# A gated FFN with seven block products for eight, GpSimd sums, and modulation on TensorE

## The chip, the cores and the metric

The kernel runs on one core of one Trainium2 chip. The metric is the device time of one execution in microseconds (us); less is better.

## The reference, cut to what matters

One inference step of a two-layer trunk for 128 context tokens and 512 latent tokens, D_MODEL 1024, all in float32. The change touches two parts of it: the up-projection of the FFN, 1024 to 2 x 2816, and the modulation vectors, six of 1024 per layer and condition.

```python
def adaln_params(cond, w_mod, b_mod):
    m = jax.nn.silu(cond) @ w_mod + b_mod
    return [t[:, None, :] for t in jnp.split(m, 6, axis=-1)]
def modulate(x, g, shift, scale):
    return rmsnorm(x, g) * (1 + scale) + shift
def conv_ffn(h, lp):
    gate, val = jnp.split(h @ lp["w_up"], 2, axis=-1)
    gate = dwconv(gate, lp["ffn_conv_w"], lp["ffn_conv_b"], FFN_CONV_PAD_L)
    return (jax.nn.gelu(gate) * val) @ lp["w_down"]
def layer(x, cond, lp, ctx):
    sh1, sc1, g1, sh2, sc2, g2 = adaln_params(cond, lp["w_mod"], lp["b_mod"])
    mix, ctx_out = token_mixers(modulate(x, lp["norm1_g"], sh1, sc1), lp, ctx)
    x = x + g1 * mix
    x = x + g2 * conv_ffn(modulate(x, lp["norm2_g"], sh2, sc2), lp)
    return x, ctx_out
```

## The kernel before, in words

Activations lie feature by feature: a chunk is 128 features in the partitions by 640 token columns (128 context, 512 latent), and 1024 features are eight chunks. TensorE works in a reduced float32 format, so every operand is split in a high and a low part, and `mm3` (358) makes three matmuls of each product: high by high, high by low, low by high. ScalarE writes the high part, VectorE the low one by a subtraction. `gemm` (367) makes one output chunk for half of the tokens (320 columns): 8 blocks of 128 input features x 3 matmuls into one of three PSUM banks `G`.

The FFN (`ffn`, 1355) goes over 22 pairs of a gate chunk and a value chunk. The first three gates are made by `first` (380) as h comes out of the norm. For every other chunk `wload` (287) fetches 512 KB of weights through a ring of two places and splits them. A gate chunk is copied out by ScalarE (`ffn_gate`, 1325), convolved and put through GeLU (`ffn_gelu`, 1341: one pass of ScalarE, two of VectorE, two of ScalarE), multiplied by the value bank (VectorE, 1385) and split. After a group of pairs (`FF_GROUPS`: 8, 8 and 6) `staggered` (1257) multiplies that group's part of W_down: eight output chunks by two halves, the last two chunks half by half, and `residual` (1247) adds the bank times the gate g2 to x, which stays in SBUF through the FFN.

The modulation vectors are made in three ways. Those of the first norm of layer 0 are part of `start` (1428). The second norm's shift and scale of layer 0 are made by `mods` (451) on TensorE: silu(c) is the stationary operand, four column tiles of 32 take four 512-column strips of w_mod at a time, in eight steps, then four transposes. The other eight vectors are made by `mods_rows` (516) on VectorE: for each of 128 (chunk, condition) pairs a row of w_mod times silu(c) is summed along 1024 columns. `mod_stream` (1594) does this for seven of the eight, within the FFN of layer 0: g2 of layer 0, then the six of layer 1; the other, g1 of layer 0, is in the attention stream.

What sets the order: TensorE's is the order of the Python text. `drive` (239) steps several generators by a model time of TensorE; `yield` gives a stream's next time or a mark that it waits for. The side streams (attention, recurrent mixer, modulation) go before the main one when they are due. The other engines and SP's DMA queue are ordered by a scheduler by priority: `soon` raises what frees a bank. Places in SBUF are handed out by hand from two pools, `F` (22 of 648 columns) and `R` (38).

The core of the modulation by rows, lines 532 to 537:

```python
for i in range(2):
    with self.soon(self.MLOW):
        nc.vector.scalar_tensor_tensor(
            out=self.S, in0=w.ap, scalar=1.0, in1=self.cb[i].ap, op0=ALU.mult, op1=ALU.mult,
            accum_out=self.mod[:, l, j, i : i + 1],
        )
```

## Time and profile before

| what | us |
|---|---|
| three runs | 2415.4 to 2415.9, median 2415.58 |
| profiled execution: span from the first to the last instruction | 2408.8 |
| median of the runs less that span | 6.8 |
| TensorE busy | 2377.8 |
| VectorE busy | 1596.7 |
| ScalarE busy | 1006.4 |
| GpSimd busy | 17.9 |

The profile has the span of the profiled execution and no total beside it; 6.8 us lie between the span and the median of the runs. Busy time is the union of an engine's instructions. TensorE's matmuls overlap (one lasts about 0.31 us and the next starts 0.15 us later), so what a matmul costs is read from the distance between starts.

### The profile page before, as it was taken

How to read it: one execution, taken by the hardware profiler on the slowest of the kernel's cores; microseconds unless marked ns; L12 is line 12 of the kernel's file. 1: busy time of each engine (PE TensorE's matmuls, PEld its weight loads, DVE VectorE, ACT ScalarE, POOL GpSimd, SP SyncE). 2: the span in 40 equal slices, each digit the busy share in tenths (PEclk: the TensorE clock that was granted, in tenths of full speed). 3: DMA queues.
4: the chain of work that ended last, by engine and by line, in shares of the span. 5: the costliest groups of instructions: out<-in, count | busy, mean ns of one | idle time of the engine just before them, and what ended most of it. 6: DMA issues, size and time to landing. Idle time of an engine off the chain costs nothing.

```text
span 2408.8 us, 41835 instructions
## 1 busy us (share of the span) xinstructions
PE 2377.8 (99%) x16847; PEld 2301.7 (96%) x16847; DVE 1596.7 (66%) x3054; ACT 1006.4 (42%) x1958; POOL 17.9 (1%) x190
## 2 busy tenths in 40 slices
PE   8999999999999999999999999999999999999998
PEld 7899999998999999999999999999889999999998
DVE  6588878766766667686756688777568564344345
ACT  4237565733334322313343566565233343133232
POOL 0000000000000000000000000000000000000000
PEclk8999999999999999999999999999999999999999
DMA  8752222222452444354423222222227212222222
GB/s 284 237 191 73 83 79 76 88 75 79 146 183 75 138 140 151 130 167 148 147 87 131 89 92 70 83 85 87 69 68 230 80 62 71 79 76 73 79 68 76
DMA packets 124961, 267.73 MB, mean 111 GB/s; under 512 B 12240, under 2 KB 45536, under 8 KB 124768
## 3 DMA queue, kind: packets, MB, share of 16 engines
q1 hardware_dynamic: 124768, 265.07, 33.2%
q8 instruction: 132, 2.16, 0.4%
q14 instruction: 61, 0.50, 0.1%
HBM read 236.95 MB, written 28.07 MB: 110 GB/s over the span
## 4 chain that ended last, share of the span: by engine, by line
PE 86%; DVE 6%; ACT 3%; DMA 3%; issue 2%; SPq 0%; DVEq 0%; ACTq 0%
PE g L273 72%; PE s L273 4%; PE tb L273 4%; PE pv L273 3%; PE tb L277 3%; DVE wl L299 1%; DMA f<-in_wmodt 1%; DVE s L534 1%; ACT f L1091 1%; PE pv L277 1%; DMA f<-in_wmod 0%; DMA wr<-in_woc 0%; DVE f L1252 0%; ACT f L913 0%; DVE r L616 0%
## 5 line engine op out<-in xcount | busy, mean ns | idle before, releaser
L273 PE MATMUL g<-r,wh 128*128 128x320 f32 (+1 forms) x7920 | 1768.5, 312 | 2.9 <-ACT f L1148 0.9
L273 PEld LDWEIGHTS g<-r,wh 128*128 128x128 f32 x7920 | 1316.6, 188 | 20.5 <-issue 13.1
L273 PE MATMUL g<-r,wl 128*128 128x320 f32 (+1 forms) x3960 | 1222.3, 309 | 2.7 <-DVE wl L299 2.7
L273 PEld LDWEIGHTS g<-r,wl 128*128 128x128 f32 x3960 | 745.1, 188 | 3.8 <-DVE wl L299 3.8
L299 DVE TENSOR_TENSOR wl<-wr,wh 128x1024 fp32r<-128x1024 f32 (+2 forms) x291 | 334.8, 1151 | 224.5 <-ACT wh L296 219.6
L296 ACT CAST wh<-wr 128x1024 fp32r<-128x1024 f32 (+2 forms) x201 | 194.2, 966 | 494.9 <-PE g L273 424.4
L1252 DVE SCALAR_TENSOR_TENSOR f<-g,mod,f 128x128 f32<-128x128 f32 (+3 forms) x192 | 78.3, 435 | 138.7 <-PE g L273 138.6
L534 DVE SCALAR_TENSOR_TENSOR s<-f 128x1024 f32<-128x1024 f32 x128 | 157.2, 1228 | 15.8 <-DMA f<-in_wmodt 11.3
L891 DVE TENSOR_REDUCE sm<-s 128x1 f32<-128x640 f32 (+3 forms) x104 | 92.8, 892 | 89.1 <-PE s L273 88.6
L273 PE MATMUL g<-r 128*128 128x322 f32 (+3 forms) x632 | 124.2, 315 | 1.4 <-ACT f L1166 1.0
L273 PE MATMUL g<-wh,r 128*128 128x256 f32 x576 | 107.7, 282 | 0.0
L273 PEld LDWEIGHTS g<-r 128*128 128x128 f32 x632 | 100.4, 190 | 5.6 <-ACT f L1091 2.1
L1385 DVE TENSOR_TENSOR f<-f,g 128x320 f32<-128x320 f32 x88 | 42.5, 486 | 91.7 <-PE g L273 56.1
L659 ACT CAST r<-f 128x640 fp32r<-128x640 f32 (+2 forms) x98 | 70.3, 720 | 65.7 <-PE s L273 27.0
L273 PEld LDWEIGHTS g<-wh,r 128*128 128x128 f32 x576 | 90.4, 188 | 3.4 <-issue 3.4
L273 PE MATMUL s<-k,r 128*128 128x320 f32 (+3 forms) x448 | 92.3, 326 | 0.9 <-ACT k L787 0.9
L660 DVE TENSOR_TENSOR r<-f,r 128x640 fp32r<-128x640 f32 (+2 forms) x98 | 79.1, 812 | 15.8 <-ACT r L659 8.4
L913 ACT ACTIVATE f<-s,sm,rs 128x640 f32<-128x640 f32 (+1 forms) x80 | 63.5, 796 | 62.0 <-DVE sm L895 44.9
L1348 DVE SCALAR_TENSOR_TENSOR f<-f,vec 128x641 f32<-128x641 f32 x88 | 77.8, 887 | 13.6 <-ACT f L1346 8.4
L913 ACT ACTIVATE f<-s,sm 128x384 f32<-128x384 f32 (+2 forms) x80 | 45.6, 577 | 92.8 <-DVE sm L900 71.0
L273 PE MATMUL g<-wl,r 128*128 128x256 f32 x288 | 81.1, 282 | 0.0
L277 PE MATMUL tb<-ident,f 128*128 128x128 f32 x576 | 79.7, 272 | 0.0
(202 smaller groups left out, 2472.6 us busy)
## 6 DMA issues: line engine op xcount, KB each, us to landing
wr<-in_wup SPq DMA_DIRECT2D x84, 512.0 KB, 3.2
wr<-in_win SPq DMA_DIRECT2D x77, 512.0 KB, 3.3
f<-in_wmodt SPq DMA_DIRECT2D x64, 512.0 KB, 4.1
f<-in_wmod SPq DMA_DIRECT2D x64, 256.0 KB, 4.6
wr<-in_wdown SPq DMA_DIRECT2D x32, 512.0 KB, 3.4
wr<-in_wqkv SPq DMA_DIRECT2D x24, 512.0 KB, 3.6
g_kept<-f SPq DMA_DIRECT2D x32, 320.0 KB, 2.3
f<-g_kept SPq DMA_DIRECT2D x32, 320.0 KB, 3.7
```

Source lines behind the costliest of these rows:

```text
L273: self.nc.tensor.matmul(**kw)
L277: self.nc.tensor.transpose(out, in_, self.ident)
L296: nc.scalar.copy(wh[:, :n], raw[:, :n])
L299: self.sub_engine().tensor_tensor(out=wl[:, o : o + c], in0=raw[:, o : o + c], in1=wh[:, o : o + c].bitcast(F32), op=ALU.subtract)
L534: nc.vector.scalar_tensor_tensor(out=self.S, in0=w.ap, scalar=1.0, in1=self.cb[i].ap, op0=ALU.mult, op1=ALU.mult, accum_out=self.mod[:, l, ...
L659: nc.scalar.copy(xh[:, :n], t[:, :n])
L660: (eng or nc.vector).tensor_tensor(out=xl[:, :n], in0=t[:, :n], in1=xh[:, :n].bitcast(F32), op=ALU.subtract)
L891: nc.vector.tensor_reduce(out=m_[:, lo:hi], in_=src, axis=AX.XY if hi - lo == 1 else AX.X, op=ALU.max)
L913: nc.scalar.activation(out=p[:, :n].rearrange("p (a c) -> p a c", a=2) if hi - lo == 1 else p[:, o : o + n], in_=src if hi - lo == 1 else ...
L1252: self.nc.vector.scalar_tensor_tensor(out=dst[:, lo:hi], in0=b[:, lo - c0 : hi - c0], scalar=self.mod[:, l, gate + m, i : i + 1], in1=src[ ...
L1348: nc.vector.scalar_tensor_tensor(out=g[:, :n], in0=gp[:, k : k + n], scalar=fw(k), in1=g[:, :n], op0=ALU.mult, op1=ALU.add)
L1385: nc.vector.tensor_tensor(out=gp[:, lo:hi], in0=gp[:, lo:hi], in1=b, op=ALU.mult)
```

## The change

The 2 x 2 block form of a pair's product: the weights of gate j and value j by the two halves of the input features, times h by halves of the features and of the tokens. Eight block products become seven, with sums of weight blocks and of h made before (by GpSimd) and sums of the products made after (by VectorE, from the banks). Three pairs of each layer stay plain (`PLAIN`). Six PSUM banks serve the products in turn. The groups become five of 5, 4, 4, 4 and 5 pairs. x no longer stays in SBUF during the FFN: it is stored at its start, read again by every group and stored by all but the last. Two weights of the down-projection are split before the group's last pair ends (`lead_weights`), and their products take all but the last block first (`gemms`). Seven modulation vectors go through `mods` on TensorE: g2 of layer 0 in its up-projection, layer 1's in the down-projection stages of layer 0's first four groups, 16 chunks (shift and scale) or 8 (a gate) at a time.

```diff
-FF_GROUPS = ((0, 8), (8, 8), (16, 6))
+FF_GROUPS = ((0, 5), (5, 4), (9, 4), (13, 4), (17, 5))
+PLAIN = 3
...
+    def gemms(self, jobs, xs, evac):
+        banks = [self.G.popleft() for _ in jobs]
+        n = len(xs)
+        for ks in (range(n - 1), (n - 1,)):
+            for (m, half, w), bank in zip(jobs, banks):
...
+                for k in ks:
+                    s = slice(k * P, (k + 1) * P)
+                    self.mm3(b, [p[:, s] for p in w], [p[:, lo:hi] for p in xs[k]], k == 0, k == n - 1)
+                    yield 0
+                if k == n - 1:
+                    evac(m, half, b)
...
-    def mods(self, ahead=2):
+    def mods(self, l, v, ahead=2):
+        n = 8 if v % 3 == 2 else 16
+        yield from self.mods_columns(l, 8 * v, n, ahead)
...
+    def mods_columns(self, l, c0, n, ahead):
+        acc, trp = self.S[:, 0], self.S[:, 1]
+        q, w = n // 4, n * P // 4
         def load(k):
+            src = self.io["wmod2"][l, k * P : (k + 1) * P, c0 * P : (c0 + n) * P]
             ws = []
+            for j in range(0, 4, 512 // w):
+                t = self.F.get()
+                nc.sync.dma_start(out=t[:, :512], in_=src[:, j * w : j * w + 512])
...
         for k in range(KC):
             ws = q_.popleft()
+            for j in range(4):
+                o = j * w % 512
                 self.matmul(
+                    w / 2.2e3, out=acc[32 * j : 32 * j + 32, :w], lhsT=self.cond[:, k], rhs=ws[j * w // 512][:, o : o + w],
                     start=(k == 0), stop=(k == KC - 1), tile_position=(0, 32 * j),
                 )
...
+    def sums_of_h(self, l):
+        nc, sub = self.nc, ALU.subtract
+        for k, x in enumerate(self.x):
+            nc.sync.dma_start(out=self.io["xm"][k], in_=x[:, :T])
...
+                    nc.scalar.activation(out=th, in_=th, func=AF.Identity, bias=self.mod[:, l, 24 + k, i : i + 1])
+        for g in range(2):
+            b11, b21, b12, b22 = (self.hf[half, g + 2 * r] for half in range(2) for r in range(2))
+            for out, in0, in1 in ((b11, b12, b11), (b12, b22, b12), (b22, b22, b11), (b21, b21, b22)):
+                self.sum_engine.tensor_tensor(out=out[:, :T], in0=in0[:, :T], in1=in1[:, :T], op=sub)
...
+    def staggered(self, l, src, xs, gate, chunk, after, early, done=None, ahead=None, lead=None):
+        if lead:
+            n0 = len(lead)
+            cs = [chunk(m) for m in range(n0)]
+            jobs = [(m, half) for m in range(n0) for half in range(2)]
...
+            yield from self.gemms([(m, half, lead[m]) for m, half in jobs[:3]], xs, evac)
+            yield from self.gemms([(m, half, lead[m]) for m, half in jobs[3:]], xs, evac)
...
+    def sum_engine(self):
+        return self.nc.gpsimd
+    def pair_weights(self, l, j):
+        nc, e = self.nc, self.sum_engine
...
+        nc.sync.dma_start(out=b[:, 2:4], in_=self.io["wup"][l, j].rearrange("p (a c) -> p a c", a=2))
+        nc.sync.dma_start(out=b[:, 0:2], in_=self.io["wup"][l, NFF + j].rearrange("p (a c) -> p a c", a=2))
...
+        a11, a12, a21, a22 = (b[:, i] for i in range(4))
+        e.tensor_tensor(out=s1, in0=a21, in1=a22, op=ALU.add)
+        e.tensor_tensor(out=a21, in0=a11, in1=a21, op=ALU.subtract)
+        e.tensor_tensor(out=s2, in0=s1, in1=a11, op=ALU.subtract)
+        e.tensor_tensor(out=s4, in0=a12, in1=s2, op=ALU.subtract)
...
+    def parts(self, ws, n):
+        x, h, lo = ws[n]
+        with self.soon(self.WSOON):
+            self.nc.scalar.copy(h, x)
+            self.nc.vector.tensor_tensor(out=lo, in0=x, in1=h.bitcast(F32), op=ALU.subtract)
...
+    def product(self, n, ws, then):
+        bank = self.pair_banks[0]
+        self.pair_banks.rotate(-1)
+        b = bank[:, :H2]
+        for i in range(4):
+            s = slice(i * P, (i + 1) * P)
+            self.mm3(b, [w[:, s] for w in ws[n][1:]], self.pair_operand(n, i), i == 0, i == 3)
+            yield 0
+        self.parts(then, n)
+        return b
+    def pair(self, l, j, ws, then, gv, during):
...
+        p1 = yield from self.product(1, ws, then)
+        with self.soon():
+            nc.scalar.copy(a, p1)
+        add(b, a, (yield from self.product(6, ws, then)))
+        add(c, b, (yield from self.product(7, ws, then)))
+        during()
+        p5 = yield from self.product(5, ws, then)
+        o = 2 + H2
+        add(gp[:, o : o + H2], c, p5)
+        add(b, b, p5)
+        p4 = yield from self.product(4, ws, then)
+        add(gp[:, 1 : 1 + SEQ], c[:, :SEQ], p4[:, :SEQ])
+        add(gp[:, 130 : 130 + H2 - SEQ], c[:, SEQ:], p4[:, SEQ:])
+        self.ffn_gelu(l, j, gp)
+        add(a, a, (yield from self.product(2, ws, then)))
+        add(b, b, (yield from self.product(3, ws, then)))
+        nc.vector.tensor_tensor(out=gp[:, :T], in0=gp[:, :T], in1=ab[:, :T], op=ALU.mult)
+        self.halves(gp, gv)
...
+            def chunk(m):
+                x = self.F.get()
+                nc.sync.dma_start(out=x[:, :T], in_=io["xm"][m])
...
+                ahead = lambda: prepare_first(c0 + nch)
+                def done(m, x):
+                    nc.sync.dma_start(out=io["xm"][m], in_=x[:, :T])
+                    self.F.put(x)
...
     def mod_stream(self):
-        yield ("h", 0, 1, 1), self.AFTER
-        self.get_cond()
-        yield from self.mods_rows(0, 5, self.PACE[2])
-        yield ("ffn", 0), 0
-        for v in range(6):
-            yield from self.mods_rows(1, v, self.PACE[3])
+        yield ("up", 0), 2
+        yield from self.mods(0, 5)
+        for g, v in ((0, 0), (1, 2), (2, 3), (3, 5)):
+            yield ("down", 0, g), 0
+            yield from self.mods(1, v)
```

`pair_weights` of pair j + 1 is called at the start of pair j, except for the first pair of a group, whose weights are fetched, summed and in part split (`prepare_first`) before the last two chunks of the down-projection in front of it.

## Rows read from the trace of the kernel before

**Rows 1.** The page's part 1, busy time by engine.
```profile
PE 2377.8 (99%) x16847; PEld 2301.7 (96%) x16847; DVE 1596.7 (66%) x3054; ACT 1006.4 (42%) x1958; POOL 17.9 (1%) x190
```

**Rows 2.** Chain that ended last, second layer's FFN (start us, us, what).
```profile
1940.97 411.32 PE g L273 x2809
```

**Rows 3.** Windows (busy: PE, PEld, VectorE, ScalarE, GpSimd): layer 1's FFN; a down-projection stage.
```profile
1940.00:2355.00 415.00, 414.99 (x2834) 414.69 (x2833) 173.78 (x233) 135.18 (x221) 5.40 (x55) 1.00 0.22 72
2040.00:2099.00 59.00, 59.00 (x404) 58.98 (x404) 21.88 (x36) 9.88 (x11) 0.29 (x3) 1.00 0.23 72
```

**Rows 4.** Chain, where a modulation piece runs on TensorE today.
```profile
64.07 2.84 PE g L273 x24
...
83.51 1.00 PE s L273 x8
84.51 3.03 PE tb L273 x24
...
110.54 0.44 PE s L277 x4
```

**Rows 5.** Groups by shape, whole run: mean ns of one stands behind the comma.
```profile
L1348 DVE SCALAR_TENSOR_TENSOR f<-f,vec 128x641 f32<-128x641 f32 x88 | 77.8, 887 | 13.6 <-ACT f L1346 8.4
...
L660 DVE TENSOR_TENSOR r<-f,r 128x640 fp32r<-128x640 f32 x76 | 61.9, 818 | 7.8 <-PE g L273 3.9 <-ACT r L659 3.9
...
L659 ACT CAST r<-f 128x640 fp32r<-128x640 f32 x76 | 55.0, 726 | 49.6 <-DVE f L1130 26.9 <-PE s L273 14.1 <-DMA f<-o_kept 4.7
...
L1385 DVE TENSOR_TENSOR f<-f,g 128x320 f32<-128x320 f32 x88 | 42.5, 486 | 91.7 <-PE g L273 56.1 <-ACT f L1352 35.6
...
L1252 DVE SCALAR_TENSOR_TENSOR f<-g,mod,f 128x320 f32<-128x320 f32 x56 | 30.7, 549 | 83.2 <-PE g L273 83.2
...
L1252 DVE SCALAR_TENSOR_TENSOR f<-g,mod,f 128x192 f32<-128x192 f32 x56 | 22.8, 408 | 0.0
...
L1252 DVE SCALAR_TENSOR_TENSOR f<-g,mod,f 128x128 f32<-128x128 f32 x64 | 22.3, 349 | 51.9 <-PE g L273 51.9
L299 DVE TENSOR_TENSOR wl<-wr,wh 128x512 fp32r<-128x512 f32 x32 | 22.0, 688 | 2.9 <-ACT wh L296 2.3
...
L296 ACT CAST wh<-wr 128x512 fp32r<-128x512 f32 x32 | 19.8, 620 | 32.7 <-PE g L273 24.7 <-DMA wr<-in_woc 4.0 <-DVE f L1183 3.8
```

**Rows 6.** VectorE in order of time (start us, us).
```profile
1960.69 0.48 DVE L1385 TENSOR_TENSOR f<-f,g 128x320 f32<-128x320 f32 x1
1961.09 1.22 DVE L299 TENSOR_TENSOR wl<-wr,wh 128x1024 fp32r<-128x1024 f32 x1
```

**Rows 7.** Groups by shape: the row sums of the modulation.
```profile
L534 DVE SCALAR_TENSOR_TENSOR s<-f 128x1024 f32<-128x1024 f32 x128 | 157.2, 1228 | 15.8 <-DMA f<-in_wmodt 11.3 <-DMA f<-cond_rows 2.7
...
L534 DVE DVE_READ_ACCUMULATOR s<-f 128x1 f32 x128 | 17.9, 140 | 0.0
```

**Rows 8.** Groups by shape, GpSimd.
```profile
L406 POOL MEMSET cond<- 128x256 f32 x1 | 0.3, 311 | 0.0
masks.py:199 POOL TENSOR_SCALAR_AFFINE_SELECT ident<-ident 128x128 f32<-128x128 f32 x1 | 0.3, 292 | 0.0
...
L405 POOL MEMSET ones<- 128x128 f32 x1 | 0.2, 204 | 0.0
```

**Rows 9.** Window where that modulation piece loads (last: clock, DMA share, GB/s).
```profile
90.00:100.00 10.00, 10.00 (x82) 7.64 (x84) 7.78 (x22) 3.22 (x7) 0.00 (x0) 1.00 0.95 327
```

**Rows 10.** Chain at a change of group, first layer.
```profile
1177.03 0.84 ACT wh L296
...
1180.98 4.08 PE g L273 x26
```

**Rows 11.** TensorE's waits, first layer's output projection and FFN.
```profile
PE g L273 <- DVE r L660: 0.4, 1, 0.4
```

**Rows 12.** Order of time, a DMA issue on SP.
```profile
1002.05 0.55 SPq L525 DMA_DIRECT2D f<-in_wmodt  x1
```

**Rows 13.** DMA issues by line (median us to landing).
```profile
wr<-in_wdown SPq DMA_DIRECT2D x14, 384.0 KB, 3.0
```

More of the change, by code (lines that the diff above doesn't have):

```diff
@@ L378, in gemm, with lead_weights @@
         return b
+    def gemms(self, jobs, xs, evac):
[3 more added lines that the diff above has]
+            for (m, half, w), bank in zip(jobs, banks):
+                lo, hi = self.cols(half)
+                b = bank[:, : hi - lo]
+                for k in ks:
[4 more added lines that the diff above has]
+                    evac(m, half, b)
+        self.G.extend(banks)
+    def lead_weights(self, src, i):
+        k2 = self.K2.rearrange("p a b -> p (a b)")
+        n = src.shape[-1]
+        raw = self.F.get()
+        self.nc.sync.dma_start(out=raw[:, :n], in_=src)
+        h, lo = (k2[:, o : o + n] for o in (2 * i * T, (2 * i + 1) * T))
+        with self.soon(self.WSOON):
+            self.split(raw, h, lo, n)
+        self.F.put(raw)
+        return h, lo
     def first(self, l, w, ws, evac):
@@ new lines, in sum_parts, with last_sum @@
+    def sum_parts(self, n):
+        for g in range(2):
+            b = self.hsum[n, g]
+            h, lo = self.R.get(), self.R.get()
+            self.split(b, h, lo)
+            self.F.put(b)
+            self.hsum[n, g] = (h, lo)
+    def last_sum(self):
+        nc = self.nc
+        for g in range(2):
+            b = self.hsum.pop((4, g))
+            for i in range(2):
+                h, lo = (x[:, H2:T] for x in self.h[2 * g + i])
+                t = b[:, i * H2 : (i + 1) * H2]
+                nc.scalar.copy(h, t)
+                nc.vector.tensor_tensor(out=lo, in0=t, in1=h.bitcast(F32), op=ALU.subtract)
+            self.F.put(b)
@@ L1255, in residual, with evac @@
             )
-    def staggered(self, l, src, xs, gate, chunk, after, early):
+    def staggered(self, l, src, xs, gate, chunk, after, early, done=None, ahead=None, lead=None):
         late = self.LATE if after is not None else 2
-        for m in range(KC - late):
+        n0 = 0
+        if lead:
+            n0 = len(lead)
+            cs = [chunk(m) for m in range(n0)]
+            jobs = [(m, half) for m in range(n0) for half in range(2)]
+            def evac(m, half, b):
+                with self.soon():
+                    self.residual(l, cs[m], cs[m], b, m, half, gate)
+                if after is not None:
+                    self.square(cs[m], m, half)
+            yield from self.gemms([(m, half, lead[m]) for m, half in jobs[:3]], xs, evac)
+            yield from self.gemms([(m, half, lead[m]) for m, half in jobs[3:]], xs, evac)
+            if done is not None:
+                for m in range(n0):
+                    done(m, cs[m])
+        for m in range(n0, KC - late):
             w = self.wload(src(m))
@@ L1284, in staggered @@
         cs = [chunk(m) for m in ms]
+        if ahead is not None:
+            ahead()
         for half in range(2):
@@ L1294, in staggered @@
                 after(half)
+        if done is not None:
+            for x, m in zip(cs, ms):
+                done(m, x)
         self.R.put(*low)
@@ L1355, in ffn, with halves @@
+    def halves(self, gp, gv):
+        xh, xl = self.R.get(), self.R.get()
+        self.split(gp, xh, xl)
+        self.F.put(gp)
+        gv.append((xh, xl))
     def ffn(self, l):
         nc, io = self.nc, self.io
-        gates = [self.ffn_gate() for j in range(3)]
+        gates = [self.ffn_gate() for j in range(PLAIN)]
         ws = self.wide + [self.wload(io["wup"][l, 2])]
@@ L1364, in ffn, with prepare, prepare_first @@
             self.ffn_gelu(l, j, gp)
+        self.sums_of_h(l)
+        self.mark("up", l)
         hs = self.h
-        for c0, nch in FF_GROUPS:
-            gv = []
+        self.raw_f = None
+        self.pair_banks = deque([*self.G, *self.TB, self.PV])
+        pw = {}
+        def prepare(j):
+            pw[j] = self.pair_weights(l, j)
+            return pw[j]
+        def prepare_first(j):
+            self.raw_turn = 0
+            if self.raw_f is None:
+                self.raw_f, self.raw_s = self.F.four(), [self.F.get() for _ in range(3)]
+            ws = prepare(j)
+            for n in (1, 6, 7):
+                self.parts(ws, n)
@@ L1380, in ffn @@
-                w = self.wload(io["wup"][l, NFF + j])
-                for half in range(2):
-                    lo, hi = half * H2, (half + 1) * H2
-                    b = yield from self.gemm(w, 0, hs, lo, hi)
-                    with self.soon():
-                        nc.vector.tensor_tensor(out=gp[:, lo:hi], in0=gp[:, lo:hi], in1=b, op=ALU.mult)
-                    yield 0
-                xh, xl = self.R.get(), self.R.get()
-                self.split(gp, xh, xl)
-                self.F.put(gp)
@@ L1393, in ffn @@
+                if then is None:
+                    during = lambda: lead.extend(self.lead_weights(src(m), m) for m in range(2))
+                yield from self.pair(l, j, pw.pop(j), then, gv, during)
             last = c0 + nch == NFF
```

162 lines of the change are left out of this document (114 added, 48 removed).

## The prediction

> **What bounds the kernel now.** I read the page's totals first, to see whether any engine is full: TensorE is busy for 99% of the span, VectorE for 66%, GpSimd for 1% [rows 1]. A busy TensorE can still be waiting on its inputs, so the chain that ended last comes next: in the second layer's FFN it is one unbroken piece of 2,809 matmuls in 411.32 us, with no other engine between them [rows 2]. That is 0.1464 us per matmul, and every matmul taken out of the FFN is worth just that. The windows say what slack stands beside it: in that stretch the granted clock is 1.00 (2.4 GHz), VectorE works 174 of 415 us, GpSimd 5, DMA moves 72 GB/s; in a down-projection stage VectorE works 22 of 59 us [rows 3]. So the FFN is TensorE's, and the other engines have room. The question is whether they still have it after the change.
>
> **TensorE: what goes.** A pair was 2 outputs x 2 token halves x 8 blocks x 3 matmuls = 96. Seven products of 4 blocks x 3 are 84. 38 pairs x 12 = 456 matmuls of 320 columns fewer, at 0.1464: **-66.8 us**. A pair takes 12.30 us instead of 14.05.
>
> **TensorE: what comes.** Five modulation pieces move to TensorE (16, 8, 16 and 8 chunks of the second layer's, 8 of the first's); one that runs there today gives the price. There a step has eight records in 1.00 us, and the 24 matmuls behind it take 3.03 instead of 2.84: 1.19 us per step [rows 4]. Eight steps and four transposes (0.44) are about 10.0 us for 16 chunks. For 8 chunks the moving operand is half as wide; the step lies between 0.60 (all of it scales) and 1.19 (nothing does). I take 0.78, nearer to scaling, since the records are long because of their 512 columns: 8 x 0.78 and two transposes, 6.5 us. Two of the first and three of the second: **+39.5 us** (+35 to +50). Net on TensorE: -27.3.
>
> **VectorE in the up-projection** does the most new work; prices in [rows 5]. Per pair: seven block splits at 0.688 = 4.82; six adds of 320 columns from a bank at 0.486 = 2.92, two more of 128 and 192 at no more than 0.349 + 0.408 = 0.76; two convolution steps at 0.887 = 1.77; product and split at 0.818 = 1.64. Sum 11.91 us against TensorE's 12.30: 97%, where it was 2 x 1.22 (the 1,024-column split [rows 6]) + 2 x 0.486 + 1.77 + 1.64 = 6.8 of 14.05. It fits, and a little better than the sum says: queued instructions start before the last one ends (one of 0.48 us starts at 1960.69, the next at 1961.09 [rows 6]). The last pair of a group splits no next weights, which lets VectorE catch up. Six banks let TensorE run some products ahead of late adds. I put this at nothing; if the cover goes, each 0.1 us over 12.30 costs 3.8 us in 38 pairs. ScalarE: even with seven splits at 0.620 = 4.3 us on top of today's third of the time (135 of 415 us [rows 3], 4.0 of 12.30) it is at 8.3 of 12.30: hidden.
>
> **VectorE elsewhere.** 112 of the 128 row sums go, with their accumulator reads: 112 x (1.228 + 0.140) = 153 us [rows 7]. It was beside TensorE's work, so it gains nothing by itself; it only makes room. Two more groups per layer mean 2 x 2 x 8 residual passes of 1.31 us (0.349 + 0.408 + 0.549), 42 us of VectorE, in stages where it is a third busy [rows 3]: nothing.
>
> **GpSimd.** No row shows it adding two tensors. Its memset of 128 columns takes 204 ns, of 256 columns 311: 0.84 ns a column written, and 0.10 us of start. A pass that also reads one tensor takes 292 for 128: 0.69 more per column read [rows 8]. So 512 columns lie between 0.53 us (writing alone) and some 1.4 (three times the write); I take 0.10 + 512 x (0.84 + 2 x 0.69) = 1.2 us, 4.9 per pair of 12.30, in an engine that is idle. The memsets of the gate's edges now queue behind the sums, but the first write into that gate comes after four products (7.0 us): covered. The eight sums of h (640 columns, 1.5 us each, 12 us per layer) lie beside three plain value chunks, 144 matmuls or 21 us.
>
> **DMA.** This is where the moved step lands. The change stores x and reads it again in every group, and brings each modulation chunk into a down-projection stage. A stage of four pairs with 16 chunks on SP's queue has 32 loads of 256 KB (8.4 MB), 8 loads and up to 8 stores of x (5.2 MB), 8 weight blocks (2.1 MB) and the next pair's weights (1.0 MB): 16.7 MB. TensorE needs 192 x 0.1464 + 10.0 = 38.1 us for it. The piece that runs today drew 327 GB/s at a DMA share of 0.95 while TensorE stayed 100% busy [rows 9], so 327 is about what there is: 51 us, 13 too many. Two of the eight steps are loaded ahead (2.1 MB, 6.4 us), which leaves 6.6 us each for two such stages; the two with 8 chunks need 12.5 MB, 38 us against 34.6, less 3.2 ahead: nothing. **+13 us** (0 to +34; below zero nothing, since no transfer gets shorter). In layer 1 a stage moves 8.3 MB in 28.1 us, 296 GB/s: it just fits.
>
> **Group changes.** A group's last pair ends in a chain of VectorE, ScalarE, VectorE before the down-projection may read it. Today's costs 4 us in the chain (1177.01 to 1180.98) [rows 10] and only 0.4 us of TensorE's waiting [rows 11]. The new order puts three jobs of 9 matmuls (3.95 us) ahead of that block; the chain is 0.49 + 0.82 + 0.73 + 0.82, 2.9 us. Ten changes instead of six at about 0.5 us: **+5 us** (0 to +15).
>
> **Sum.** 2408.8 (span) - 27.3 + 13 + 5 = 2399.5; the profile lists no total beside its span, so I add the 6.8 us between it and the median of the runs, 2415.58: 2406.3. With rounding, **2407 us**, 0.35% faster.
>
> **Rivals.** (a) *GpSimd and VectorE shut each other out* (slower). Place: the up-projection, wherever a sum of GpSimd meets a VectorE instruction with two inputs from SBUF. Speaking against it: nothing, since GpSimd has never read a tensor beside VectorE here; [rows 8] hold memsets and two small set-up passes. If they exclude each other, a pair holds 4.82 + 1.77 + 1.64 = 8.2 us of such VectorE work and 4.9 of GpSimd: 13.1 us, 0.8 over TensorE's 12.30 when the bank adds all fall beside GpSimd, and 4.5 when none does (11.91 + 4.9). It decides from a sum of 1.02 us on, (12.30 - 8.2) / 4. 28 of the 38 pairs have the next pair's sums beside them (the other ten are made in the stage before): 22 to 126 us. Most adds can fall beside, so 0.8 to 1.2: **2430 us**. This is what the Trainium skill says in "SBUF — State Buffer", Who interferes with whom: a VectorE instruction with two SBUF inputs and a GpSimd instruction that reads SBUF share one read port, and the second to start is blocked for the whole of the first. By that rule the sum is 2430, by the engines' separate rows 2407; no row here shows it either way.
> (b) *The transfers bound the first layer's down-projections*: no prefetch helps because the first loads queue behind x, and SP issues 58 DMAs at up to 0.55 us [rows 12], 32 of 38 us. Then 2 x 13 + 2 x 4 = 34 instead of 13: **2428 us**, with 2415 to 2440 about it. For it: bytes; against it: today's piece at the same share held nothing up.
> (c) *SP's order*: the store of chunk m waits for its residual, and behind it waits the next weights' load. If the order puts it so, the next chunk starts 0.55 + 0.4 + 3.0 (landing of such a block [rows 13]) + 0.62 + 0.69, 5.3 us, late: four chunks in eight stages, +170 us, **2577 us**. Against it: SP's waits today are for buffers, not for stores, and a load that is ready can be put first.
>
> **How the numbers follow.** About 0.2% (4.8 us) can be told from no change. Forecast 0.53 (2391 to 2416: 0.48 of it faster, 0.05 the same); (a) 0.25 (0.03 the same, 0.22 slower); (b) 0.18 (0.08 and 0.10); (c) 0.04 slower. Faster 0.48, same 0.16, slower 0.36: signs mix, so the forecast's own range stands above. The range starts where DMA and group changes cost nothing (2388) and takes in most of (a) and (b): 2390 to 2440.
>
> **What would show it.** Right: some 456 fewer matmuls of 320 columns, 0.146 us apart, and a pair of pair stages at 12.3 us; GpSimd at about 1.2 us per sum; VectorE over 90% busy in the up-projection but not waited for; waits of TensorE for modulation loads of some 13 us. Wrong by (a): VectorE's splits of 512 columns far above 0.69 us or gaps before them while GpSimd runs, and TensorE waiting for VectorE in the up-projection. Wrong by (b): TensorE waiting for loads in the first layer's down-projections, at a DMA share near 1. Wrong by (c): idle stretches of 5 us at every chunk. The argument falls altogether if the FFN's TensorE pitch is no longer 0.146 us.

## The result, and the profile after

The changed kernel takes **2490.0 us** (2486.9 to 2491.9, 4 runs) against 2415.5 for the kernel before on the same chip: ratio 1.0308 [1.0294, 1.0323]. It is slower by 3.1% where I forecast 2407 us, and the time lies above the range of 2390 to 2440.

The profiled execution is 2489.0 us, with a span of 2487.0 us. TensorE's and GpSimd's totals, from the page's part 1 of the changed kernel, answer to [rows 1]:

```profile
PE 2391.0 (96%) x16725; PEld 2268.8 (91%) x16725; DVE 1810.3 (73%) x3439; ACT 1095.3 (44%) x2177; POOL 291.2 (12%) x358
```

The matmul count is as the diff says: 16,847 - 456 + 334 = 16,725. So the work went and the time did not: TensorE is at 96% where it was at 99%. Set against the kernel before by the norm ahead of each FFN in the two traces, the stretch from the first layer's to the second layer's grew by 76 us (1178.8 to 1254.6). From there to the end it grew by 6 (489.1 to 494.8), where 19 x 12 matmuls fewer should have made it 33 us shorter. What lies ahead of the first layer's FFN became 3 us shorter.

Next, windows of the changed kernel, with the columns of [rows 3]: a pair in the second layer, a down-projection stage of the first layer (from the product 1 of a group's last pair to that of the next group's first pair), and the same stretch in the second layer.

```profile
core 0: us, PE busy (x) PEld busy (x) DVE busy (x) ACT busy (x) POOL busy (x), PEclk, DMA share, GB/s
...
2224.00:2237.90 13.90, 13.90 (x97) 13.90 (x96) 13.90 (x20) 6.73 (x14) 6.87 (x8) 1.00 0.21 68
831.80:903.40 71.60, 65.67 (x387) 52.81 (x387) 28.29 (x58) 14.38 (x24) 7.08 (x10) 0.93 0.73 236
2251.80:2292.60 40.80, 37.34 (x244) 36.93 (x243) 27.59 (x53) 12.30 (x22) 4.37 (x7) 0.96 0.60 193
```

Three things are to be seen. A pair lasts 13.90 us, not 12.30, and VectorE is busy in all of it. TensorE's row also looks full there, but that is because it runs ahead on six banks and pays later, in one wait near the end of a group (six of the ten groups have one, of 2.7 to 3.5 us). The first layer's stage lasts 31 us longer than the second layer's, at 236 GB/s on the mean. And the granted clock is 0.93 and 0.96 there: behind most of its gaps TensorE runs for 3.4 or 6.8 us at 1.2 GHz, where it had run at 2.4 GHz before the gap (over the whole run the mean clock is 0.983, and 0.996 in the kernel before).

What TensorE waited for, changed kernel, whole run (us, times, longest); in the kernel before, [rows 11] have 0.4 us in all for the first layer's output projection and FFN:

```profile
PE g L275 <- DVE f L1537: 13.5, 4, 3.5
PE g L275 <- DVE f L1348: 12.7, 5, 3.8
PE g L275 <- ACT wh L298: 8.5, 4, 2.9
PE g L275 <- ACT f L1458: 7.3, 2, 4.4
PE g L275 <- ACT r L755: 7.0, 4, 3.1
PE g L275 <- DVE r L659: 5.6, 4, 2.2
PE s L275 <- DMA f<-in_wmod: 5.4, 8, 2.2
```

L1537 are the bank adds of the pairs: that is VectorE, late at the end of a group. Three of the five waits for L1348 (the residual, whose x came late; 7.7 us), those for L298 (weights) and part of in_wmod are the first layer's down-projections short of data. L1458, L659 and the other two waits for L1348 are the start of the FFN stage.

Why VectorE needs 13.90 us is in its own rows beside GpSimd's. The order of time in the changed kernel, one pair (start us, us, engine line):

```profile
2230.33 1.30 POOL L1493 TENSOR_TENSOR f<-wr 128x512 f32<-128x512 f32 x1 [4.76 <-DVE wl L1509]
...
2230.64 1.54 DVE L1509 TENSOR_TENSOR wl<-f,wh 128x512 fp32r<-128x512 f32 x1
...
2231.71 1.63 POOL L1494 TENSOR_TENSOR wr<-wr 128x512 f32<-128x512 f32 x1
...
2232.10 1.92 DVE L1469 SCALAR_TENSOR_TENSOR f<-f,vec 128x641 f32<-128x641 f32 x1
...
2233.30 1.88 POOL L1495 TENSOR_TENSOR f<-f,wr 128x512 f32<-128x512 f32 x1
...
2233.94 0.47 DVE L1537 TENSOR_TENSOR f<-f,g 128x320 f32<-128x320 f32 x1
...
2234.34 1.39 DVE L1509 TENSOR_TENSOR wl<-f,wh 128x512 fp32r<-128x512 f32 x1
...
2236.85 0.68 DVE L1509 TENSOR_TENSOR wl<-f,wh 128x512 fp32r<-128x512 f32 x1
```

The first sum of GpSimd ends at 2231.63. The split that VectorE began beside it ends at 2232.18, 0.55 us later, and so lasts 1.54 us instead of the 0.68 of the split at 2236.85. The convolution step waits in the same way for the second sum (its end 2233.34, the step's 2234.02), and the third sum lasts 1.88 us because it waits for that step. The two take turns, each for a whole instruction. This holds throughout the trace: all 100 weight splits (L1509) and all 26 convolution steps that begin during a weight sum of GpSimd end after it (a split 0.55 us, a step 0.69 us after). The bank add at 2233.94, whose second input comes from a PSUM bank, is not stretched (0.47 us), and all 70 adds from a bank that begin during a weight sum end before it; but this one stands behind the stretched step in VectorE's queue.

### The profile page after: what moved, and what is told of

It is laid out like the page before. It is cut to its first block, busy times and chain, and to the rows that moved or that the text cites. A ratio compares the mean times of both kernels' runs of the same rounds, so it can differ in the third digit from the quotient of the medians.

```text
span 2487.0 us, 43303 instructions
## 1 busy us (share of the span) xinstructions
PE 2391.0 (96%) x16725; PEld 2268.8 (91%) x16725; DVE 1810.3 (73%) x3439; ACT 1095.3 (44%) x2177; POOL 291.2 (12%) x358
## 3 DMA queue, kind: packets, MB, share of 16 engines
q1 hardware_dynamic: 157888, 316.47, 39.5%
## 5 line engine op out<-in xcount | busy, mean ns | idle before, releaser
L275 PE MATMUL g<-r,wh 128*128 128x320 f32 (+1 forms) x5736 | 1305.7, 316 | 25.6 <-ACT wh L298 8.5
L275 PEld LDWEIGHTS g<-r,wh 128*128 128x128 f32 x5736 | 959.8, 190 | 67.4 <-issue 35.7
L275 PE MATMUL g<-r,wl 128*128 128x320 f32 (+1 forms) x2868 | 892.8, 311 | 3.4 <-DVE wl L301 3.4
L275 PEld LDWEIGHTS g<-r,wl 128*128 128x128 f32 x2868 | 544.5, 190 | 6.0 <-DVE wl L301 6.0
L275 PE MATMUL g<-r,k 128*128 128x320 f32 (+2 forms) x1520 | 265.9, 321 | 33.8 <-DVE f L1537 13.5
L301 DVE TENSOR_TENSOR wl<-wr,wh 128x1024 fp32r<-128x1024 f32 (+2 forms) x227 | 232.2, 1024 | 90.0 <-ACT wh L298 84.1
L275 PEld LDWEIGHTS g<-r,k 128*128 128x128 f32 x1520 | 239.9, 197 | 42.6 <-DVE f L1537 14.5
L1348 DVE SCALAR_TENSOR_TENSOR f<-g,mod,f 128x128 f32<-128x128 f32 (+3 forms) x288 | 115.1, 436 | 185.6 <-PE g L275 153.3
L298 ACT CAST wh<-wr 128x512 fp32r<-128x512 f32 (+2 forms) x137 | 106.8, 784 | 245.3 <-PE g L275 140.9
L275 PE MATMUL g<-r 128*128 128x322 f32 (+2 forms) x628 | 125.6, 320 | 6.5 <-DVE f L1348 5.0
L755 ACT CAST r<-f 128x640 fp32r<-128x640 f32 (+2 forms) x110 | 78.8, 723 | 90.9 <-PE s L275 27.0
L1509 DVE TENSOR_TENSOR wl<-f,wh 128x512 fp32r<-128x512 f32 x116 | 95.6, 827 | 4.5 <-ACT wh L1508 4.4
```

The costliest lines, as they stand in the source:

```text
L275: self.nc.tensor.matmul(**kw)
L298: nc.scalar.copy(wh[:, :n], raw[:, :n])
L301: self.sub_engine().tensor_tensor(out=wl[:, o : o + c], in0=raw[:, o : o + c], in1=wh[:, o : o + c].bitcast(F32), op=ALU.subtract)
L755: nc.scalar.copy(xh[:, :n], t[:, :n])
L1348: self.nc.vector.scalar_tensor_tensor(out=dst[:, lo:hi], in0=b[:, lo - c0 : hi - c0], scalar=self.mod[:, l, gate + m, i : i + 1], in1=src[ ...
L1509: self.nc.vector.tensor_tensor(out=lo, in0=x, in1=h.bitcast(F32), op=ALU.subtract)
```

## Experiments

Theory A: GpSimd's sums and VectorE's two-input instructions shut each other out. Theory B: the loads of the moved modulation crowd the first layer's down-projections. The rival to A was theory C, that 13.9 us is VectorE's work and its waits whoever makes the sums. Ratios are against runs of the kernel before made beside each experiment, with 95% intervals. Those read 2411 to 2413 us, and 2415.5 beside the changed kernel, so a difference from 2490.0 us becomes 3 to 4 us smaller when each kernel is set against its own neighbour. In the code, only the lines that carry an edit are shown, and three dots mark what is left out.

**All sums on VectorE** (e1)

```
 def sum_engine(self):
-    return self.nc.gpsimd
+    return self.nc.vector
```

> All sums (four per pair, and those of h) on VectorE, nothing else changed. Theory A: a pair takes 13.9 us because VectorE's two-input instructions and GpSimd's sums hold each other up; VectorE's own work is 11.9. Then the 512-column splits come back to 0.69 us, and a pair with the next pair's sums beside it costs 11.9 + 4 x 0.69 = 14.7 us, less a little overlap: 14.2 to 14.8. 28 such pairs x 0.3 to 0.9 us more, less some 10 us of waiting at the two stage starts: 2480 to 2510 us. Theory C: the 13.9 us are VectorE's work and its waits on other engines, whoever makes the sums; then a pair becomes 13.9 + 2.8 = 16.7 us and the time some 2560 us.

Measured: 2453.6 us, 1.0171 [1.0126, 1.0216], so 36 us faster than the changed kernel (33 with each against its own neighbour), and below the times of both theories. The copy of product 1 out of its bank starts every 12.3 us (12.38, 12.30, 12.34 in the second group). Windows of two pairs, columns as above:

```profile
2199.90:2212.20 12.30, 12.30 (x86) 12.30 (x85) 11.90 (x23) 6.88 (x13) 0.36 (x4) 1.00 0.22 70
2212.20:2224.50 12.30, 12.30 (x86) 12.30 (x85) 12.09 (x23) 6.87 (x13) 0.23 (x3) 1.00 0.38 121
```

VectorE makes four more sums and needs less time: 12.0 of 12.30, and TensorE sets the period. C's 16.7 us did not come, and A's own 14.2 to 14.8 was too high as well, for durations overlap in VectorE's queue. In order of time, VectorE of this run:

```profile
2193.30 0.68 DVE L1509 TENSOR_TENSOR wl<-f,wh 128x512 fp32r<-128x512 f32 x1
2194.02 0.69 DVE L1493 TENSOR_TENSOR f<-f 128x512 f32<-128x512 f32 x1
2194.63 0.55 DVE L1537 TENSOR_TENSOR f<-f,tb 128x128 f32<-128x128 f32 x2
2195.09 0.69 DVE L1509 TENSOR_TENSOR wl<-wr,wh 128x512 fp32r<-128x512 f32 x1
2195.70 0.69 DVE L1494 TENSOR_TENSOR f<-f 128x512 f32<-128x512 f32 x1
2196.30 0.48 DVE L1537 TENSOR_TENSOR f<-f,pv 128x320 f32<-128x320 f32 x1
```

A sum or split of 0.69 us is followed some 0.60 us after its start. This distance between starts, the pitch, is its price in a full queue, and it is less than VectorE loses to the same sum on GpSimd, as the next run shows.

**No sums** (e2)

```
-e.tensor_tensor(out=s1, in0=a21, in1=a22, op=ALU.add)
...
+s1, s2, s4 = a22, a11, a12
```

> The four sums of each weight pair and the sums of h are left out (the products are taken of the plain blocks, so the output is another one); all splits, products, adds and loads stay. Theory A: no GpSimd tensor reads, so the splits are 0.69 us, VectorE needs 11.9 us per pair and TensorE 12.3 sets the period: 28 pairs x 1.5 us and some 10 to 20 us at the two stage starts go, 2425 to 2445 us. Theory C: the period stays near 13.9 us and only the stage starts gain: 2470 to 2480 us.

Measured: 2443.5 us, 1.0129 [1.0074, 1.0184]; the pair is 12.3 us and VectorE is busy 10.7 of it:

```profile
2191.70:2204.00 12.30, 12.30 (x86) 12.30 (x85) 10.75 (x20) 7.07 (x13) 0.29 (x3) 1.00 0.21 72
```

So VectorE's own work is 10.7 us by the trace, where my sum of durations was 11.91, and GpSimd's four sums added (13.9 - 10.7) / 4 = 0.8 us each. Between this run and the one before lie 10 us (two runs of each): all that the sums cost on VectorE.

**Sums of h alone on VectorE** (e6)

```
-self.sum_engine.tensor_tensor(out=out[:, :T], ...
+nc.vector.tensor_tensor(out=out[:, :T], ...
```

> Only the sixteen sums of h go from GpSimd to VectorE, the sums of the weights stay on GpSimd. Theory A: the period of the pairs stays at 13.9 us; the gap of 4.7 and 3.2 us at the two stage starts, where ScalarE's queue waits for GpSimd, goes with some of its neighbours: 2474 to 2484 us. If the h sums were the larger part of what the run with all sums on VectorE gave (36 us): 2450 to 2460 us.

Measured: 2483.4 us (two runs, 2478 and 2488), 1.0297 [1.0275, 1.0319]; the pair stays at 13.9 us. That is 7 us less than the changed kernel, or 3 with each against its own neighbour, and two runs 10 us apart cannot tell it from nothing. What the traces show is that TensorE's two waits for L1458, 7.3 us at the starts of the two FFN stages, are gone. How they came about shows there in the changed kernel (order of time, then ScalarE's waits):

```profile
783.52 3.65 POOL L684 TENSOR_TENSOR f<-f 128x640 f32<-128x640 f32 x2
...
784.23 0.72 ACT L755 CAST r<-f 128x640 fp32r<-128x640 f32 x1
...
784.85 0.42 ACT L1458 COPY f<-g 128x320 f32<-128x320 f32 x1
...
785.32 0.62 PE L275 MATMUL g<-r,wh 128*128 128x320 f32 x2 [4.42 <-ACT f L1458]
```

```profile
ACT r L755 <- POOL f L684: 7.8, 5, 3.4
```

ScalarE's split of a sum of h (L755) waits for GpSimd, the copy that empties a bank (L1458) stands behind it in ScalarE's queue, and TensorE waits 4.42 us for that bank.

**No modulation pieces on TensorE** (e3)

```
-yield from self.mods_columns(l, 8 * v, n, ahead)
+if (l, v) == (0, 3):
+    yield from self.mods_columns(l, 8 * v, n, ahead)
+else:
+    self.nc.vector.memset(self.mod[:, l, 8 * v : 8 * v + n], 0.1)
```

> The five modulation pieces that the change put on TensorE are left out with their loads (the vectors are filled with a constant, so the output is another one). Theory B: the first layer's down-projection stages pay for the loads as well as for the matmuls, some 74 us by the difference between the two layers' stages: 2410 to 2425 us. Rival: only the TensorE time of the pieces, 39.5 us as forecast, and the rest of the first layer's loss comes from the pairs: 2445 to 2455 us.

Measured: 2414.8 us, 1.0013 [1.0001, 1.0024]: 75 us less (72 with each against its own neighbour), as B said. The first layer's four stages last 45.8, 40.7, 40.9 and 42.2 us, much as those of the second do, where the changed kernel's last 71.6, 50.8, 64.4 and 50.6.

**The kernel before, with the five pieces on TensorE** (e4)

```
-yield from self.mods_rows(1, v, self.PACE[3])
+yield from self.mods(1, v)
```

> The kernel before with its 112 row sums of VectorE replaced by the same five pieces on TensorE, spread over the first layer's FFN, where little else is loaded. If the pieces cost only their TensorE time, 39.5 us: 2450 to 2460 us, with VectorE's busy time down by some 150 us. If each step costs more than the forecast wherever it stands (the matmuls themselves or their loads), 2475 to 2490 us.

Measured: 2448.5 us, 1.0149 [1.0097, 1.0202]: 36.7 us more than the 2411.8 beside it (two runs, 7 us apart). Spread over a stretch with little traffic, the pieces cost their TensorE time.

**The pieces without most of their loads** (e5)

```
-ws = q_.popleft()
+ws = once or q_.popleft()
```

> The changed kernel with the five modulation pieces on TensorE as they are, but the loads of seven of each piece's eight steps left out (all steps multiply by the first step's block, so the output is another one). Leaving the pieces out altogether gave 75 us, the same pieces in the kernel before cost 37. If the other 38 us are transfers that the down-projections and the pieces wait for, this run is at 2445 to 2460 us. If they are the pieces' places in TensorE's order, with whatever they put behind them, it stays at 2475 to 2490 us.

Measured: 2455.2 us, 1.0180 [1.0162, 1.0199]: the loads are worth 31 to 35 us. So of the 72 to 75 us some 37 are matmuls and the rest is crowding, most of it by these loads.

**The second layer only, sums on VectorE and on GpSimd** (h1, h2; `ffn_plain` is the FFN of the kernel before, and the modulation is made as there)

```
-yield from self.ffn(l)
+yield from (self.ffn if l else self.ffn_plain)(l)
```

> The first layer's FFN and the modulation as in the kernel before (plain pairs, row sums on VectorE), the second layer's FFN with seven products and all sums on VectorE. From the stretches: the second layer's FFN took 461 us with sums on VectorE against 479 in the kernel before, so 18 us less than the kernel before of the same call, -0.6 to -0.9%. If VectorE became the bound without GpSimd too, or the first layer paid for the new places of buffers: no gain.

> The same with the sums of the second layer on GpSimd, as the change has them. Theory A: pairs of 13.9 us use up all that the seven products give; the second layer's FFN took 4 us more than the kernel before's there: 0 to 6 us slower than the kernel before, and 20 to 25 us slower than with the sums on VectorE. Rival: the loss of the changed kernel is all in the first layer, where modulation stands, and GpSimd's sums cost no time by themselves: 15 to 20 us faster than the kernel before, the same as with the sums on VectorE.

Measured: 2394.9 us, **0.9931 [0.9918, 0.9943]**, with the sums on VectorE; 2419.1 us, 1.0028 [1.0018, 1.0039], with the sums on GpSimd. Where no modulation stands, the engine of the sums alone decides the sign, by 24 us in 19 pairs. The first is faster than both kernels, by 0.7% than the kernel before; of the 33 us that TensorE saves there, it keeps 17.

**What in GpSimd's work holds VectorE up** (f4: fills, which read nothing; f5: one input read)

```
-e.tensor_tensor(out=s1, in0=a21, in1=a22, op=ALU.add)
...
+for s in (s1, a21, s2, s4):
+    e.memset(s, 0.5)
+    e.memset(s, 0.25)
```

```
+for s, a in ((s1, a22), (a21, a21), (s2, a11), (s4, a12)):
+    e.tensor_scalar(out=s, in0=a, scalar1=0.5, scalar2=None, op0=ALU.mult)
```

> The run with plain pairs in the first layer and GpSimd's sums in the second (0.28% over the kernel before), the four weight sums of each pair replaced by eight fills of 512 columns (two per sum, by the rows of before some 0.53 us each, 4.2 us per pair), which read nothing; the output is another one, the sums of h stay. If GpSimd holds VectorE up only where it reads tensors: VectorE's splits are 0.69 us throughout, the pair is 12.3 us, some 20 us less than with sums: 2395 to 2403 us. If any work of GpSimd does it: the pair stays at 13.3 to 13.9 us, 2412 to 2419 us.

> The same with the four weight sums replaced by four multiplications by a constant on GpSimd, one tensor read each instead of two; the output is another one. If one read is enough to shut VectorE's two-input instructions out for the whole of GpSimd's instruction, each costs VectorE about what it lasts, some 0.9 us: a pair of 13.3 to 13.9 us, 2410 to 2419 us. If only two reads do it: 12.3 us, 2395 to 2403 us.

Measured: 2402.3 us, 0.9961 [0.9947, 0.9976], and 2398.4 us, 0.9945 [0.9927, 0.9963]; the pair is 12.30 us in both. Groups by shape in the second layer's pairs (count, busy us, mean ns): the splits of the run with GpSimd's sums (h2), then two groups of the fills (f4), then GpSimd's and VectorE's with one read (f5), and last one moment of f5 in order of time.

```profile
L1470 DVE SCALAR_TENSOR_TENSOR f<-f,vec 128x641 f32<-128x641 f32 x28 | 33.9, 1212 | 1.6 <-ACT f L1468 1.6
L1510 DVE TENSOR_TENSOR wl<-f,wh 128x512 fp32r<-128x512 f32 x40 | 32.4, 810 | 0.0
L1510 DVE TENSOR_TENSOR k<-f,k 128x512 fp32r<-128x512 f32 x27 | 24.5, 908 | 5.2 <-PE g L276 2.7 <-ACT k L1509 2.5
...
L1510 DVE TENSOR_TENSOR wl<-wr,wh 128x512 fp32r<-128x512 f32 x12 | 16.4, 1368 | 0.0
```

```profile
L1509 DVE TENSOR_TENSOR wl<-f,wh 128x512 fp32r<-128x512 f32 x40 | 27.5, 687 | 0.0
...
L1495 POOL MEMSET f<- 128x512 f32 x42 | 22.0, 527 | 84.0 <-DVE wl L1509 40.5 <-DVE k L1509 34.7 <-DMA f<-in_wup 8.7
```

```profile
L1495 POOL TENSOR_SCALAR f<-f 128x512 f32<-128x512 f32 x24 | 38.8, 1623 | 30.2 <-DVE k L1508 14.2 <-DVE wl L1508 8.3 <-DMA f<-in_wup 7.7
...
L1508 DVE TENSOR_TENSOR k<-f,k 128x512 fp32r<-128x512 f32 x27 | 20.4, 756 | 1.7 <-PE g L276 1.6
...
L1508 DVE TENSOR_TENSOR wl<-wr,wh 128x512 fp32r<-128x512 f32 x12 | 8.3, 688 | 0.0
```

```profile
2089.64 1.49 POOL L1495 TENSOR_SCALAR f<-f 128x512 f32<-128x512 f32 x1 [1.40 <-DVE wl L1508]
2090.34 0.69 DVE L1508 TENSOR_TENSOR wl<-wr,wh 128x512 fp32r<-128x512 f32 x1
```

Fills stretch nothing (687 ns, as alone). Four instructions per pair that read one tensor, 1.6 us each, stretch one group of splits to 756 ns on the mean, where the sums stretched it to 908, and leave another at 688, where the sums stretched it to 1368. Of the 58 weight splits that begin during such an instruction 36 end before it, as the one at 2090.34 does. Only the two-input sums shut VectorE out for their whole length. The Trainium skill, "SBUF — State Buffer", Who interferes with whom, has the mechanism: one shared read port, no conflict with a GpSimd that only writes, none for a VectorE instruction with one SBUF input. The bank adds at 0.47 us and the fills agree with it. Where the Trainium skill has any GpSimd instruction that reads SBUF contend there, the measurement decides: one with a single read delays some splits by up to 0.4 us and does not block for its whole length.

**Crowding: rate or order of the queue?** (e8: stores of x on GpSimd's queue; e9: no such stores in the first layer)

```
 def done(m, x):
-    nc.sync.dma_start(out=io["xm"][m], in_=x[:, :T])
+    nc.gpsimd.dma_start(out=io["xm"][m], in_=x[:, :T])
```

```
+    if l > 0:
         nc.sync.dma_start(out=io["xm"][m], in_=x[:, :T])
```

> The changed kernel with the stores of x after every chunk of a down-projection (all but the last of each layer) issued by GpSimd's queue instead of SP's; nothing else changed, the same bytes move. If the loads of modulation and weights wait in SP's queue behind stores that wait for VectorE's residual (11.5 us of SP's waits in the first such stage), the first layer's stages shorten: 2460 to 2478 us. If the transfer rate is the limit: 2483 to 2492 us.

> The changed kernel with those stores left out in the first layer only (the residual of earlier groups is then lost, so the output is another one): 10.5 MB fewer in four stages. If SP's order is the cause, about the time of the run with the stores on another queue, 2460 to 2478 us. If the rate is: 10.5 MB at 236 to 327 GB/s are 32 to 44 us, of which the 35 us that the loads cost can give back at most most: 2455 to 2465 us, and below the run on the other queue by 15 us or more.

Measured: 2492.8 us, 1.0330 [1.0311, 1.0349], and 2465.4 us, 1.0216 [1.0196, 1.0237]. The first lies 1 us above what the rate theory allowed, but tells less than it was meant to. SP's waits in the first such stage, in the changed kernel and then in e8:

```profile
SPq L1640 <- DMA x_middle<-f: 11.8, 5, 4.5
SPq L1652 <- DVE f L1348: 11.5, 8, 4.2
```

```profile
SPq L1640 <- DMA x_middle<-f: 29.0, 5, 7.6
```

The stores' wait for VectorE (L1652) left SP, and the load of the next x (L1640) then waited 17 us longer for the stores' landing: the wait moved. Leaving the stores out gave 21 to 25 us, less than my 32 to 44 for the bytes alone; it is 27 us below e8, as the rate theory wanted. That stage in e9:

```profile
831.70:892.30 60.60, 59.79 (x388) 49.01 (x387) 29.66 (x57) 13.44 (x23) 5.68 (x9) 1.00 0.71 235
```

It moves 235 GB/s on the mean without the stores and 236 with them. That leans to the rate, but the stores' bytes and the waits for them left together here, and in e8 the waits only moved.

**The pieces beside the pairs** (m2: sums on GpSimd; n2: on VectorE)

```
-for g, v in ((0, 0), (1, 2), (2, 3), (3, 5)):
-    yield ("down", 0, g), 0
+for g, v in ((1, 0), (2, 2), (3, 3), (4, 5)):
+    yield ("pairs", 0, g), 0
```

> The changed kernel with the four pieces of the second layer's modulation placed in the stretches of pairs of groups 1 to 4 of the first layer, not in the down-projections; same loads, same matmuls. If transfer rate in the down-projections is what the loads are short of, their 35 us go; and since VectorE sets 13.9 us per pair there, TensorE has 1.6 us free in most of 16 pairs, up to 25 us, for the pieces' matmuls: 2430 to 2458 us. If it is the order of SP's queue, which waits for VectorE's splits in the pairs as well: 2475 us or more.

> The same with all sums on VectorE (2453.6 us with the pieces in the down-projections). Transfer rate: 30 to 38 us less, and none of the pieces' matmuls is hidden, since TensorE sets the 12.3 us of a pair: 2415 to 2425 us, 0 to 0.6% over the kernel before. SP's order: 2440 us or more.

Measured: 2435.2 us, 1.0091 [1.0071, 1.0111], and 2409.5 us, 0.9989 [0.9979, 0.9999]: 55 us less than the changed kernel and 44 less than e1 (52 and 45 with each against its own neighbour), from the place of four pieces alone, with every byte and matmul kept. The second lies below its range. The 44 are the cleaner figure: in m2 VectorE sets the pace of the pairs, and part of the pieces' matmuls hides beside it. With the sums on VectorE and the pieces beside the pairs, both causes are gone, and the kernel takes the time of the kernel before. In windows of m2, the first down-projection and the group of pairs behind it:

```profile
831.20:878.10 46.90, 46.90 (x319) 46.69 (x319) 28.63 (x54) 13.80 (x23) 5.07 (x6) 1.00 0.58 189
878.10:923.90 45.80, 45.80 (x314) 38.58 (x313) 41.51 (x57) 20.07 (x37) 22.02 (x21) 1.00 0.73 249
```

The stage of 71.6 us is one of 46.9, TensorE has no gap in either stretch, and the clock stays at 1.00. Crowding in one stage is shown as the cause; whether rate or the waits in SP's queue set the limit inside such a stage is not settled.

**The start of the FFN stage** (f1: bias additions later; f2: left out; f3: residual ahead of the norm; f6: the norm's chunks in turn; f1 and f2 are edits of h1, f3 adds to f1 and f6 adds to f3)

```
-bias=self.mod[:, l, 24 + k, i : i + 1])
+bias=late[:, 2 * k + i : 2 * k + i + 1])
```

```
-nc.scalar.activation(out=th, in_=th, func=AF.Identity, bias=self.mod[:, l, 24 + k, i : i + 1])
```

```
-with self.soon(self.MSOON):
+with self.soon(1200):
     self.modulated(l, w, k, half, t, half * H2)
```

```
+self.in_turn(l, w, k, half)
 self.modulated(l, w, k, half, t, half * H2)
```

> The run with plain pairs in the first layer and sums on VectorE in the second, with one edit: the 24 bias additions that make the sums' h on ScalarE take their bias from a copy that is made only when the first products of half 0 have left their banks, so that none of them stands in ScalarE's queue ahead of the norm. If those additions hold up the norm, the gaps of 2.46, 2.82, 1.91 and 1.05 us at the start of the second layer's FFN and the stretch at half clock behind them go, 6 to 11 us: 2384 to 2389 us, 1.1 to 1.3% under the kernel before. If the gaps have another cause: no change, 0.7% under it. If they only move the wait (the first sums of h then come late for product 6): 0.5 to 0.7%.

> The same kernel with the 24 bias additions left out instead (the sums are then of h without its shift, so the output is another one). If the additions, wherever they stand, are what the start of the stage pays: 2384 to 2389 us, and equal to the run that moves them when the move hides them all; if the gaps have another cause: 2395 us.

> The run with the bias additions moved, and one more edit: VectorE's norm instructions of the second layer's FFN get a lower priority than the residual of the last chunk, so that both residuals stand among them, as in the kernel before, and not behind all 32. If the wait for the residual opens the gap: 2386 to 2390 us, 1.1 to 0.9% under the kernel before. If what TensorE waits for is the last of the norm's low parts, which still stand at the end in one row: no change, 0.6 to 0.7% under it.

> The same with the norm's chunks in turn too: the first instruction of chunk k reads its scale from a cell that is written only after the low part of chunk k-2 is made (32 small instructions on VectorE more). The kernel before gets this order from the buffers that its chunks take turns in; the change keeps eight of them, so the first instructions of all chunks go ahead. If that order opens the gaps of 4.86, 1.69 and 1.28 us and the half-clock stretch: 2384 to 2390 us, 0.9 to 1.1% under the kernel before. If ScalarE's part of the norm is what is late: no change, 0.6 to 0.7% under it.

Measured: 2395.5 (0.9939 [0.9926, 0.9953]), 2395.1 (0.9931 [0.9913, 0.9950]), 2395.5 (0.9928 [0.9912, 0.9943]) and 2397.6 us (0.9934 [0.9921, 0.9946]): no gain in any, and none differs from h1. TensorE's waits at the start of the stage, in h1, in f1 and in f6:

```profile
PE g L276 <- DVE r L660: 2.8, 2, 2.2
PE g L276 <- DVE f L1349: 2.5, 1, 2.5
PE g L276 <- ACT f L1457: 1.6, 1, 1.6
```

```profile
PE g L276 <- DVE r L660: 5.4, 2, 4.6
PE g L276 <- ACT f L1457: 1.4, 1, 1.4
```

```profile
PE pv L277 <- DVE f L609: 4.0, 1, 4.0
PE g L277 <- ACT k L1528: 2.4, 2, 2.0
```

The waits changed their names and kept their size. In f1, f2 and f3 the wait for the residual (L1349) is gone and the one for the norm's low parts (L660) is longer by as much or more; in f6 that one is gone and a wait for the norm's sum of squares (L609) stands in its place. These 7.5 to 9.5 us of waits, with 6.8 to 10.2 us at half clock behind them, remain without a settled cause.

## Why the prediction was wrong

**Right: TensorE's sum.** 456 matmuls went, their pitch is still 0.146 us (12.30 us for 84), and a pair takes 12.30 us once nothing else is late (e1, h1, f4). The five pieces cost 36.7 us against the 39.5 that I took from [rows 4]. That the row sums hid beside TensorE fits as well: e4 took 112 of them off VectorE and still paid 37 us, within 3 of the pieces' own price.

**Wrong: "I put this at nothing."** The step that failed is the cover of VectorE in the pairs. The 11.91 us were too much (10.7 by the trace) since the pitch is below the duration, as I had noted for one pair of rows in [rows 6] and then not used. What the step left out is that GpSimd's sums are not beside VectorE but in its way: 13.9 us per pair. GpSimd's own price was right, 1.30 us for a sum that begins unhindered against the 1.2 forecast; beside VectorE it is 1.6 to 1.9. All sums together cost 33 to 36 us more on GpSimd than on VectorE.

**Rival (a) was the mechanism, and its total came out nearly right by luck.** I let most bank adds fall beside GpSimd and came to 0.8 to 1.2 us per pair; it is 1.6 in most of the 28 pairs. Bank adds are not stretched, but an add behind a blocked split waits with it in VectorE's queue (2233.94 behind 2232.10). That would be 45 us and not 22, but not all of it reaches the total: from the first pair's product 1 to the last pair's, e1 is 17.8 us shorter in the second layer and only 8.3 in the first, 26 us in all. The likely reason, not tested by itself, is that the first layer's down-projections wait for data anyway. The rival's chance was 0.25 though nothing spoke against it but the lack of rows, and an operation that no row shows deserved more.

**Wrong: "+13 us" of DMA.** The bytes were right (16.7 MB forecast, 16.92 MB moved in the stage). The mis-sized term is the rate: I took 327 GB/s for the whole stage, and though single slices of it reach 390, it reached 236 on the mean, while loads of x waited for buffers and stores for residuals. Cost: 31 to 35 us (e5) to 45 (n2 against e1). Rival (b) said 34, and its split fits too: the four stages are 25.8, 10.1, 23.5 and 8.4 us longer than e3's; less the 10.0 and 6.5 us that I had for a piece's matmuls, this leaves 15.8, 3.6, 13.5 and 1.9, where (b) had 13 and 4.

**Wrong: one rival at a time.** (a) and (b) sit in different stages and both came true. Their prices should have been added: 2407 + 23 + 21 is 2451, already past my range.

**Not foreseen: the start of the stage.** I had the sums of h "beside three plain value chunks". On GpSimd they last 1.8 to 1.9 us each, not 1.5, and ScalarE's queue carries the wait to TensorE's banks: waits of 7 us, gone in e6. A further 11 to 13 us per layer (some 8 of gaps, and half of the half-clock stretches) has no shown cause. Group changes cost 1.2 us where TensorE sets the pace (41.6 between groups in e1 against 28.1 + 12.3), not 0.5.

**Rival (c)**, a store ahead of each load, came as 11.5 us of SP's waits in a stage, not as idle stretches of 5 us at every chunk.

The way back from the changed kernel, each run against its own neighbour: the sums on VectorE give 33 us (e1), the place of the pieces another 45 (n2), and n2 is then 3 us under the kernel before, where TensorE's own terms (-66.8 + 36.7) are 30 under it. The 27 us between are what group changes (some 10 by the 1.2 us each) and the starts of the FFN stages (22 to 26) cost; no run takes either away, and added one by one they come to more than the 27, so their sizes are estimates from waits.

## What to carry to other kernels

An engine that is idle is not free: look first at what it shares with the engine that is nearly full. Here a sum on idle GpSimd took more of VectorE's time than the same sum on VectorE. When a step is moved, price it in the stage where it lands, with all that moves there, and try another stage: the same five pieces cost 37 us spread out, and 72 to 75 us with four of them in the down-projections. And rivals that sit in different stages add; a range that holds only one of them at a time is too narrow.

## What the runs showed of the hardware

VectorE starts its next queued instruction some 0.09 us before the last one ends (0.69 us of duration, 0.60 us of pitch for 512 columns), so a sum of durations overstates a full queue: 11.91 us here for 10.7. A GpSimd sum of two tensors and a VectorE instruction with two inputs from SBUF ran strictly in turn: each of 100 splits and 26 convolution steps that began during a weight sum ended 0.55 or 0.69 us after it. A GpSimd instruction with one input only brushed VectorE (36 of 58 splits ended inside it, means of 688 to 756 ns). Most gaps of TensorE of 2 to 5 us in the changed kernel were followed by 3.4 or 6.8 us at 1.2 GHz, so that a short wait cost, by estimate, half its length again or as much again; three such gaps, of 2.3, 2.7 and 3.3 us, were not.
